# Attention scores of two heads at a time on two row halves of the array, queries turned two heads at a time

## The chip, the cores and the metric

The kernel runs on one core of one Trainium2 chip. The metric is the device time of one execution in microseconds (us), lower is better. Engines are named as in the profile: PE is TensorE's matmul, PEld its weight load, DVE is VectorE, ACT is ScalarE, POOL is GpSimd, SP is SyncE, which only issues DMAs here.

## The reference

One encoder layer on two sequences of 512 tokens, model width 1024. A normalised input is projected to queries (16 heads of 64), keys and values (4 heads of 64), the input of a state-space branch and two gates. The two branches are gated and added, an output projection and a squared-ReLU MLP follow. The change touches the attention branch alone:

```python
q = rms_norm(q.reshape(bsz, seq_len, N_HEADS, HEAD_DIM), q_gain)
k = rms_norm(k.reshape(bsz, seq_len, N_KV_HEADS, HEAD_DIM), k_gain)
...
s = jnp.einsum('nqkgd,njkd->nkgqj', qb, kw).astype(jnp.float32) * scale + bias
s = jnp.where(mask[:, None, None], s, NEG_INF)
sink_col = jnp.broadcast_to(sink_b, s.shape[:-1] + (1,))
p = jax.nn.softmax(jnp.concatenate([s, sink_col], axis=-1), axis=-1)[..., :-1]
o = jnp.einsum('nkgqj,njkd->nqkgd', p.astype(vs.dtype), vw)
```

A block of 128 queries sees its own block of keys and the two beside it, where they exist: two key blocks (256 keys) for the first and last block of a sequence, three (384 keys) for the two in the middle. A score is a product over 64 head dimensions.

## The kernel before

All matmuls split their float32 operands into a high and a low part of a faster type and add several products of the parts, so as to come near float32.

The attention stage (lines 953 to 1367) goes through 8 steps, one for each of the 4 key heads j and 2 sequences sq. A step has four units, one for each block qb of 128 queries. A unit covers the four query heads h = 0 to 3 that share key head j. Beside the unit, the step projects the queries of the next step, one tile of 128 tokens in each unit.

A tile of queries (class `Tile`) goes through these steps. `project` multiplies 24 products of 256 columns in portions. `square`, `power` and `norm` normalise each head: ScalarE squares (L1001), VectorE sums (L1005), POOL raises to the power -1/2 (L1007, L1008), VectorE multiplies into `qn` (L1012). In the kernel before, `qn` holds each head twice side by side, the second copy made by POOL (L1013). `turn` transposes each head's 128 columns (head twice) on TensorE (L1018), which gives 128 rows: the head's 64 dimensions, twice. `high` writes all 128 rows as the high part (L1023, ScalarE), and `low` writes rows 64 to 127 over with the low part (L1027, VectorE). So `queries[j, sq]` holds for each head the high part in rows 0 to 63 and the low part in rows 64 to 127.

Keys are treated alike once a step: `key_copies` (L972) makes two copies side by side on POOL, `key_turn` transposes them (L981) and writes a tile `kh` of high parts (L982) and a tile `kl` of low parts (L983), each with the same 64 dimensions in both row halves.

`scores(h)` then takes two matmuls of all 128 rows for a head (L1048): high and low queries against `kh`, and high and low queries against `kl`. Together these are all four products of the parts. The result is one PSUM bank from the pool `ps_s`, which has two banks, so the third head of a unit takes the bank of the first and the fourth that of the second.

`largest(h)` (L1052, VectorE) adds the bias, writes the scores to `p` and finds the negated row maximum; with it the score bank is free. Two instructions show in the profile: the custom operation and a read of its accumulator. `exp(h)` (L1058) is on ScalarE. The probabilities of a unit are used while the next unit runs (`prev`): `turn(i)` transposes the four heads' probabilities of key block i (L1064), `high(i)` (L1068, ScalarE) and `low(i)` (L1073, VectorE) split them, `value(i, part)` (L1080) multiplies with the values, `lower_part` (L1084) and, one unit later still, `add` (L1090, VectorE, two instructions) bring the output together.

The order on TensorE, ScalarE, VectorE and POOL is written out by hand (the manual schedule opened at L1195); an engine works off its instructions in that order. For the first part of a unit it is, in the kernel before: `scores(0)`, `largest(0)`, `rows.power`, `scores(1)`, `owed.add`, `largest(1)`, `prev.turn(0)`, `prev.high(0)`, 8 products of the projection, `prev.low(0)`, `exp(0)`, `exp(1)`, `rows.norm`, `scores(2)`, `largest(2)`, `prev.turn(1)`, `prev.high(1)`, 4 products, `value(0, 0)`, 2 products, `exp(2)`, `scores(3)`, a weight's low part, `prev.low(1)`, `value(0, 1)`, `largest(3)`, and then the third key block, 4 products, `rows.turn`, and the rest (lines 1217 to 1309). Here `rows` is the tile projected in the unit before, and `rows.turn` its transposes.

Of the kernel before, what the change touches and what calls it, by code (L numbers as in the profile page):

```python
# [11 lines left out]
F32 = mybir.dt.float32  # L12
F32R = mybir.dt.float32r
I32 = mybir.dt.int32
AF = mybir.ActivationFunctionType
ALU = mybir.AluOpType
AX = mybir.AxisListType

P = 128
# [6 lines left out]
HALF = 512  # L26
# [3 lines left out]
G = 4  # L30
HD = 64
# [32 lines left out]
def hybrid_layer(ctx, tc, x, xT, rel, onehot, early, w_qkv, w_ug, q_gain, k_gain, sink,  # L64
                 b_re, b_im, c_re, c_im, d_skip, w_glu, b_glu, w_out, ln2, w_up, w_down, out):
    nc = tc.nc
    V, S, PE, GP, SP = nc.vector, nc.scalar, nc.tensor, nc.gpsimd, nc.sync
# [12 lines left out]
    def acc():  # L80
        return ps_acc.tile([P, 512], F32, tag="acc", name="acc")

    def tps():
        return ps_t.tile([P, 512], F32, tag="tps", name="tps")

    def sps():
        return ps_s.tile([P, 512], F32, tag="sps", name="sps")
# [16 lines left out]
    ident = const.tile([P, P], F32, name="ident")  # L104
# [4 lines left out]
    gain_q = const.tile([P, 1], F32, name="gain_q")  # L109
# [161 lines left out]
    with tc.tile_pool(name="xin", bufs=2, reuse_waits="tile") as xin, tc.tile_pool(name="ssmc", bufs=1) as sc:  # L271
        def c64(name):
            return sc.tile([P, GROUPS], F32, tag=name, name=name)
# [65 lines left out]
        dt, mag, ang, kk = c64("dt"), c64("mag"), c64("ang"), c64("kk")  # L339
# [79 lines left out]
        for s in range(NSEQ):  # L419
            for c in range(3):  # L420
                out_ps[c, s] = (tps, tps, sps, sps, acc, lambda: ps_o.tile([P, 512], F32, tag="po", name="po"))[s * 3 + c]()
            for k in range(KT):
# [38 lines left out]
                for p, c in order:  # L461
                    PE.matmul(out_ps[c, s], u_w[c][p == 2][:, k, :], hT[s][p == 1][:, k, :],
                              start=k + p == 0, stop=k == KT - 1 and p == 1)
# [10 lines left out]
        for n in (1, 2, 4):  # L474
            a, b = slice(1, n + 1), slice(n + 1, 2 * n + 1)
# [46 lines left out]
    if True:  # L522
        h = hp.tile([P, NCHUNK, 2, GROUPS, NSEQ], F32, name="h")
# [429 lines left out]
    with tc.tile_pool(name="att", bufs=2, reuse_waits="tile") as ap:  # L953
        steps = [(j, sq) for j in range(N_KV) for sq in range(NSEQ)]
        weights, keys, queries, biases = {0: w_q0}, {}, {}, {}
# [12 lines left out]
                biases[j].append(bias)  # L968

        def key_copies(j, sq):  # L970
            kd = ap.tile([P, 4, 2, HD], F32, tag="qn", name="kd")
            GP.tensor_copy(kd, kn[:, sq * 4:sq * 4 + 4, j, None, :].to_broadcast([P, 4, 2, HD]))  # L972
            return kd

        def key_turn(j, sq, kd):
            kh = ap.tile([P, HALF], F32R, tag="kh", name="kh")
            kl = ap.tile([P, HALF], F32R, tag="kl", name="kl")
            keys[j, sq] = (kh, kl)
            ps = tps()
            for t in range(4):  # L980
                PE.transpose(ps[:, t * P:(t + 1) * P], kd[:, t].rearrange("p a d -> p (a d)"), ident)  # L981
            S.activation(kh, ps, AF.Copy, scale=gain_k)  # L982
            V.scalar_tensor_tensor(kl, ps, gain_k, kh.bitcast(F32), op0=ALU.mult, op1=ALU.subtract)  # L983
            queries[j, sq] = ap.tile([P, G, HALF], F32R, tag="qa", name="qa")

        class Tile:

# [20 lines left out]
                GP.tensor_tensor(self.rq, ms, neg_half[:, 0:G], op=ALU.pow)  # L1008

            def norm(self):  # L1010
                self.qn = ap.tile([P, G, 2, HD], F32, tag="qn", name="qn")
                V.tensor_mul(self.qn[:, :, 0], self.psv, self.rq[:, :, None].to_broadcast([P, G, HD]))  # L1012
                GP.tensor_copy(self.qn[:, :, 1], self.qn[:, :, 0])  # L1013

            def turn(self):
                self.pt = acc()
                for h in range(G):
                    PE.transpose(self.pt[:, h * P:(h + 1) * P], self.qn[:, h].rearrange("p a d -> p (a d)"), ident)  # L1018

            def high(self):  # L1020
                self.ptv = self.pt.rearrange("p (h t) -> p h t", h=G)
                self.dst = queries[self.key][:, :, self.t * P:(self.t + 1) * P]
                S.activation(self.dst, self.ptv, AF.Copy, scale=gain_q)  # L1023

            def low(self):
                dst = self.dst[64:128]
                V.scalar_tensor_tensor(dst, self.ptv[64:128], gain_q[64:128], dst.bitcast(F32),  # L1027
                                       op0=ALU.mult, op1=ALU.subtract)

        class Unit:  # L1030

# [9 lines left out]
                self.nmx = small.tile([P, G], F32, tag="nmx", name="nmx")  # L1041
                self.s, self.pt, self.hl = {}, {}, {}

            def scores(self, h):
                ps = self.s[h] = sps()
                qs = queries[self.j, self.sq][:, h, self.qb * P:(self.qb + 1) * P]
                for i, kk in enumerate(keys[self.j, self.sq]):
                    PE.matmul(ps[:, 0:self.nk], qs, kk[:, self.k0 * P:self.k1 * P], start=i == 0, stop=i == 1)  # L1048

            def largest(self, h):  # L1050
                hh, b0 = self.j * G + h, (self.k0 - self.qb + 1) * P
# [108 lines left out]
        def y_high(m, yr):  # L1160
            for s in range(NSEQ):
                S.copy(y_part(s, 0, m).rearrange("p (t k) -> p t k", t=T), yr[:, :, s, :])
# [36 lines left out]
        if True:  # L1199
            rows = entry()  # L1200
            for i, (j, sq) in enumerate(steps):
# [8 lines left out]
                for qb in range(NB):  # L1210
                    if 1 <= i < 3:

                        t = (i - 1) * NB + qb
# [3 lines left out]
                    cur = Unit(j, sq, qb, sums, ya)  # L1217
# [4 lines left out]
                    kd = None  # L1222
# [3 lines left out]
                        rows.power()  # L1226
                    if i == len(steps) - 1:
                        y_high(2 * qb, y_rows[2 * qb])
                    cur.scores(1)
                    if owed:  # L1230
                        owed.add()
                    cur.largest(1)
# [12 lines left out]
                    if qb == 0 and nxt:  # L1245
                        kd = key_copies(*nxt)
# [2 lines left out]
                        made = None  # L1249
                    if div:  # L1250
                        div.invert()
                    cur.scores(2)
                    cur.largest(2)
                    if i == len(steps) - 1:
                        y_low(2 * qb, y_rows[2 * qb])
# [7 lines left out]
                    if i == len(steps) - 1:  # L1263
                        y_high(2 * qb + 1, y_rows[2 * qb + 1])
                    cur.exp(2)
                    cur.scores(3)
                    if lower:
                        lower()
                        lower = None
# [632 lines left out]
    with tc.tile_pool(name="down0", bufs=2, side="right", reuse_waits="tile") as d0, \  # L1902
# [50 lines left out]
        ps = product_d(1)  # L1953
# [4 lines left out]
        ps = product_d(5, added(q3, q1, xq))  # L1958
# [5 lines left out]
        ps = product_d(6, added(q5, q5, xq))  # L1964
# [3 lines left out]
        ps = product_d(3)  # L1968
# [4 lines left out]
        ps = product_d(7)  # L1973
# [4 lines left out]
        ps = product_d(2, added(q1, q1, xq))  # L1978
# [3 lines left out]
        ps = product_d(4)  # L1982
# [77 lines left out]
```

## Time and profile before

| | us |
|---|---|
| three timed runs | 1470.78, 1468.74, 1468.35 |
| their median | 1468.74 |
| the profiled execution's own time: first to last instruction (span) | 1467.4 |
| TensorE busy in the span | 1446.3 |
| first to last start of a score matmul (L1048) | 451.4 to 675.3 |

The profiled execution is known by its span alone; the median of the timed runs lies 1.3 us above it, for what lies around the span and for the spread between runs. A row of a group names the line, engine, operation, written tile, read tiles, shape and count, then the busy time in us, the mean of one in ns, the idle time before it and what ended that. A row of the timeline begins with the start and the duration in us; several like instructions in a row are merged with their count, and then the duration runs from the first start to the last end. A matmul's duration is longer than the distance to the next matmul, since they are pipelined; the distance of two starts is what it costs TensorE.

### The profile page before, as it was taken

Reading aid. Unit: us, or ns where it says so; the run is one execution under the profiler, and the core shown is the slowest. Engines: PE = TensorE matmul, PEld = TensorE weight load, DVE = VectorE, ACT = ScalarE, POOL = GpSimd, SP = SyncE. Lnnn points to the kernel's source line nnn. Section 1 sums busy time; section 2 is a strip of 40 time slices with the busy share of each in tenths; the row PEclk is TensorE's granted clock in tenths of the full one; section 3 lists DMA queues with packets and bytes.
Section 4 is the critical chain, followed back from the end, with each engine's and each line's share of the span. In section 5 each row is a group of like instructions: output and inputs, shape, how many; then the busy total and the mean of one; then the engine's idle time right before and its main releaser. Section 6 shows DMA issues by size and latency. Waiting matters only on the chain.

```text
span 1467.4 us, 21580 instructions
## 1 busy us (share of the span) xinstructions
PE 1446.3 (99%) x7782; PEld 1234.1 (84%) x7782; DVE 1094.6 (75%) x1836; ACT 764.2 (52%) x1366; POOL 168.9 (12%) x270
## 2 busy tenths in 40 slices
PE   6999999999999999999999999999999999999998
PEld 5888888888999899987888888888888888888887
DVE  7799979975636889888974689877776588575653
ACT  5489862233426778787532355554554444333332
POOL 4111120000223333343101000000000000000000
PEclk9999999999999999999999999999999999999999
DMA  8355567259941413236964134544443894454441
GB/s 300 112 171 174 161 206 268 101 178 290 307 131 35 121 46 89 95 130 217 303 212 144 72 115 165 174 149 147 155 158 123 302 346 147 158 177 153 129 129 58
DMA packets 129239, 243.86 MB, mean 166 GB/s; under 512 B 16060, under 2 KB 59324, under 8 KB 129133
## 3 DMA queue, kind: packets, MB, share of 16 engines
q1 hardware_dynamic: 104684, 186.87, 40.4%
q10 hardware_dynamic: 21888, 46.15, 8.3%
q0 software_dynamic: 2560, 9.48, 2.0%
q8 instruction: 61, 1.00, 0.3%
q14 instruction: 46, 0.37, 0.1%
HBM read 173.20 MB, written 81.82 MB: 174 GB/s over the span
## 4 chain that ended last, share of the span: by engine, by line
PE 91%; DVE 3%; ACT 2%; DMA 1%; issue 1%; POOL 1%; SPq 0%; DVEq 0%; ACTq 0%; POOLq 0%
PE bank L115 14%; PE bank L116 14%; PE bank L117 14%; PE acc L141 11%; PE acc L724 8%; PE acc L753 5%; PE acc L115 3%; PE acc L117 3%; PE acc L116 3%; PE po L1080 2%; PE sps L604 2%; PE sps L1048 2%; PE sps L860 2%; PE tps L1064 2%; PE lag L619 1%
## 5 line engine op out<-in xcount | busy, mean ns | idle before, releaser
L116 PE MATMUL bank<-b_lo,a_hi 128*128 128x512 f32 x440 | 171.2, 389 | 0.0
L117 PE MATMUL bank<-b_hi,a_lo 128*128 128x512 f32 x440 | 171.2, 389 | 0.0
L115 PE MATMUL bank<-b_hi,a_hi 128*128 128x512 f32 x440 | 171.2, 389 | 0.0
L724 PE MATMUL acc<-w_hi,hT 128*128 128x256 f32 x768 | 165.0, 291 | 0.0
L141 PE MATMUL acc<-hT,c_hi 128*128 128x512 f32 x512 | 161.1, 394 | 0.0
L1933 ACT CAST a_hi<-d_a 128x1024 fp32r<-128x1024 f32 x55 | 58.0, 1054 | 178.1 <-PE bank L116 175.2
L1934 DVE TENSOR_TENSOR a_lo<-d_a,a_hi 128x1024 fp32r<-128x1024 f32 x55 | 67.3, 1223 | 99.4 <-ACT a_hi L1933 97.3
L724 PEld LDWEIGHTS acc<-w_hi,hT 128*128 128x128 f32 x768 | 126.7, 190 | 1.7
L141 PEld LDWEIGHTS acc<-hT,c_hi 128*128 128x128 f32 x512 | 94.6, 188 | 21.0 <-issue 2.5
L724 PE MATMUL acc<-w_lo,hT 128*128 128x256 f32 x384 | 108.2, 282 | 0.0
L141 PE MATMUL acc<-hT,c_lo 128*128 128x512 f32 x256 | 100.3, 392 | 0.0
L115 PE MATMUL bank<-act,u_hi 128*128 128x512 f32 x256 | 99.6, 389 | 0.0
L116 PE MATMUL bank<-act,u_hi 128*128 128x512 f32 x256 | 99.6, 389 | 0.0
L117 PE MATMUL bank<-act,u_lo 128*128 128x512 f32 x256 | 99.6, 389 | 0.0
L117 PEld LDWEIGHTS bank<-b_hi,a_lo 128*128 128x128 f32 x440 | 82.6, 188 | 17.3
L115 PEld LDWEIGHTS bank<-b_hi,a_hi 128*128 128x128 f32 x440 | 82.6, 188 | 17.1
L116 PEld LDWEIGHTS bank<-b_lo,a_hi 128*128 128x128 f32 x440 | 82.6, 188 | 17.1
L1058 ACT ACTIVATE p<-p,nmx 128x257 f32<-128x257 f32 (+1 forms) x128 | 72.1, 564 | 27.0 <-DVE nmx L1052 24.3
L724 PEld LDWEIGHTS acc<-w_lo,hT 128*128 128x128 f32 x384 | 73.0, 190 | 2.5
L1052 DVE CUSTOM_DVE_ANT_0 p<-sps,bias,nsink 128x256 f32<-128x256 f32 (+1 forms) x128 | 69.2, 541 | 2.9 <-PE sps L1048 0.4
L1717 ACT CAST u_hi<-s 128x512 fp32r<-128x512 f32 x64 | 39.3, 621 | 59.8 <-PE bank L116 43.1
L1934 DVE TENSOR_TENSOR b_lo<-k,b_hi 128x1024 fp32r<-128x1024 f32 x55 | 66.9, 1217 | 0.0
(387 smaller groups left out, 3622.9 us busy)
## 6 DMA issues: line engine op xcount, KB each, us to landing
d_a<-a_scr SPq DMA_DIRECT2D x55, 512.0 KB, 3.6
u_raw<-in_w_up_dram SPq DMA_DIRECT2D x32, 512.0 KB, 5.7
a_scr<-t ACTq DMA_DIRECT2D x64, 256.0 KB, 2.1
k<-in_w_down_dram SPq DMA_DIRECT2D x32, 512.0 KB, 5.7
a_scr<-a ACTq DMA_DIRECT2D x48, 256.0 KB, 3.3
c_raw<-in_w_ug_dram SPq DMA_DIRECT2D x44, 256.0 KB, 3.6
ct_scr<-ctab SPq DMA_DIRECT2D x16, 576.0 KB, 3.3
ctab_in<-ct_scr SPq DMA_DIRECT2D x32, 288.0 KB, 4.7
```

Of the source, the lines that this page charges most:

```text
L115: PE.matmul(ps, a[0], b[0], start=first, stop=False)
L116: PE.matmul(ps, a[0], b[1], start=False, stop=False)
L117: PE.matmul(ps, a[1], b[0], start=False, stop=last)
L141: PE.matmul(self.ps[s], self.w[p == 2][:, k, :], hT[s][p == 1][:, k, :], start=i % (3 * KT) == 0, stop=i % (3 * KT) == 3 * KT - 1)
L604: PE.matmul(ps[:, i * P:(i + 1) * P], bm[:, ri, g, :], u_sb[:, g, :], start=True, stop=True)
L724: PE.matmul(ps, act[p == 2][:, k, col:col + P], self.w[k // 4][p == 1][:, k % 4, :], start=i == 0, stop=i == 3 * KT - 1)
L753: PE.matmul(self.ps[s], w_g[self.m][p == 2][:, k, :], y_part(s, int(p == 1), k), start=k + p == 0, stop=k == KT - 1 and p == 2)
L1052: V.tensor_tensor_reduce(self.p[:, h, 1:1 + self.nk], self.s[h][:, 0:self.nk], biases[self.j][h][:, b0:b0 + self.nk], -1.0, nsink[:, hh:hh ...
L1058: S.activation(p, p, AF.Exp, bias=self.nmx[:, h:h + 1], scale=-1.0, accum_out=self.sums[:, h, self.qb:self.qb + 1])
L1717: S.copy(hi, src)
L1933: S.copy(hi, src)
L1934: V.tensor_sub(lo, src, hi.bitcast(F32))
```

## The change

Queries are no longer doubled. `norm` writes the four heads side by side, without POOL's copy. `turn` transposes two heads at once, so that a tile of queries takes two transposes instead of four; head 2m comes into rows 0 to 63 and head 2m + 1 into rows 64 to 127. `high` and `low` write two separate tiles of this form, each 128 rows by 256 columns. `scores(m)` now makes the scores of the heads 2m and 2m + 1: three products of 64 rows for each head (high queries with high keys, low with high, high with low), the two heads alternating, head 2m in the rows 0 to 63 of the array and head 2m + 1 in the rows 64 to 127, into two score banks. The product of the two low parts is left out.

In the written order, `scores(0)` stands where `scores(0)` stood, and covers heads 0 and 1. `scores(1)` stands where `scores(2)` stood, and covers heads 2 and 3. Nothing else is moved. The key copies have one buffer (`bufs=1`) in the place of two shared with the queries.

```diff
         def key_copies(j, sq):
-            kd = ap.tile([P, 4, 2, HD], F32, tag="qn", name="kd")
+            kd = ap.tile([P, 4, 2, HD], F32, tag="qn", name="kd", bufs=1)
...
-            queries[j, sq] = ap.tile([P, G, HALF], F32R, tag="qa", name="qa")
+            queries[j, sq] = ap.tile([P, 2, 2, HALF], F32R, tag="qa", name="qa")
...
             def norm(self):
-                self.qn = ap.tile([P, G, 2, HD], F32, tag="qn", name="qn")
-                V.tensor_mul(self.qn[:, :, 0], self.psv, self.rq[:, :, None].to_broadcast([P, G, HD]))
-                GP.tensor_copy(self.qn[:, :, 1], self.qn[:, :, 0])
+                self.qn = ap.tile([P, G, HD], F32, tag="qm", name="qn")
+                V.tensor_mul(self.qn, self.psv, self.rq[:, :, None].to_broadcast([P, G, HD]))
 
             def turn(self):
-                self.pt = acc()
-                for h in range(G):
-                    PE.transpose(self.pt[:, h * P:(h + 1) * P], self.qn[:, h].rearrange("p a d -> p (a d)"), ident)
+                self.pt = acc()[:, 0:2 * P]
+                for m in range(2):
+                    PE.transpose(self.pt[:, m * P:(m + 1) * P], self.qn[:, 2 * m:2 * m + 2].rearrange("p a d -> p (a d)"), ident)
 
             def high(self):
-                self.ptv = self.pt.rearrange("p (h t) -> p h t", h=G)
-                self.dst = queries[self.key][:, :, self.t * P:(self.t + 1) * P]
-                S.activation(self.dst, self.ptv, AF.Copy, scale=gain_q)
+                self.ptv = self.pt.rearrange("p (m t) -> p m t", m=2)
+                self.hi, self.lo = [queries[self.key][:, i, :, self.t * P:(self.t + 1) * P] for i in range(2)]
+                S.activation(self.hi, self.ptv, AF.Copy, scale=gain_q)
 
             def low(self):
-                dst = self.dst[64:128]
-                V.scalar_tensor_tensor(dst, self.ptv[64:128], gain_q[64:128], dst.bitcast(F32),
-                                       op0=ALU.mult, op1=ALU.subtract)
+                V.scalar_tensor_tensor(self.lo, self.ptv, gain_q, self.hi.bitcast(F32), op0=ALU.mult, op1=ALU.subtract)
...
-            def scores(self, h):
-                ps = self.s[h] = sps()
-                qs = queries[self.j, self.sq][:, h, self.qb * P:(self.qb + 1) * P]
-                for i, kk in enumerate(keys[self.j, self.sq]):
-                    PE.matmul(ps[:, 0:self.nk], qs, kk[:, self.k0 * P:self.k1 * P], start=i == 0, stop=i == 1)
+            def scores(self, m):
+                for e in range(2):
+                    self.s[2 * m + e] = sps()
+                tok, kk = slice(self.qb * P, (self.qb + 1) * P), slice(self.k0 * P, self.k1 * P)
+                for n, (a, b) in enumerate(((0, 0), (1, 0), (0, 1))):
+                    for e in range(2):
+                        rows_ = slice(e * 64, (e + 1) * 64)
+                        PE.matmul(self.s[2 * m + e][:, 0:self.nk], queries[self.j, self.sq][rows_, a, m, tok],
+                                  keys[self.j, self.sq][b][rows_, kk], start=n == 0, stop=n == 2)
...
-                    cur.scores(1)
                     if owed:
                         owed.add()
                     cur.largest(1)
...
-                    cur.scores(2)
+                    cur.scores(1)
                     cur.largest(2)
...
                     cur.exp(2)
-                    cur.scores(3)
```

## The prediction

> **What bounds the kernel now.** I first read the busy shares of the page, then the same shares for the stretch in which the attention steps run, 460 to 640 us, since the change touches nothing outside attention.
>
> ```profile
> span 1467.4 us, 21580 instructions
> PE 1446.3 (99%) x7782; PEld 1234.1 (84%) x7782; DVE 1094.6 (75%) x1836; ACT 764.2 (52%) x1366; POOL 168.9 (12%) x270
> ...
> 460.00:640.00 180.00, 178.66 (x1310) 166.28 (x1311) 157.83 (x418) 143.69 (x364) 63.50 (x113) 1.00 0.27 80
> ```
>
> The columns of the last line are PE, PEld, DVE, ACT, POOL, clock, DMA. TensorE is busy for 178.66 of 180 us; VectorE comes second with 157.83, or 88%. So TensorE time taken out of this stretch would come off the span, but only while VectorE keeps up, and its slack is about one part in eight. The waits of the same stretch say where VectorE already holds TensorE up:
>
> ```profile
> PEld sps L1048 <- DVE nmx L1052: 2.1, 7, 0.7
> ```
>
> The 128-row score products (L1048) wait 2.1 us in 7 cases for VectorE's row maximum (L1052), because that frees a score bank. There are only two such banks (`ps_s`, bufs=2). This small wait is the one that the change enlarges, so the order of TensorE and VectorE inside a unit (one head group, one block of 128 queries) has to be read next. Here is a unit with two key blocks (256 score columns, "narrow"), TensorE first, then VectorE:
>
> ```profile
> 594.96 0.28 PE L1048 MATMUL sps<-kh,qa 128*128 128x256 f32 x1
> ...
> 596.83 0.28 PE L1048 MATMUL sps<-kh,qa 128*128 128x256 f32 x1
> ```
>
> ```profile
> 594.57 0.76 DVE L1027 SCALAR_TENSOR_TENSOR qa<-acc,gain_q,qa 64x512 fp32r<-64x512 f32 x1 [0.41 <-ACT qa L1023]
> 595.40 0.49 DVE L1052 CUSTOM_DVE_ANT_0 p<-sps,bias,nsink 128x256 f32<-128x256 f32 x1
> 595.81 0.08 DVE L1052 DVE_READ_ACCUMULATOR2_ANT nmx<- 128x1 f32 x1
> 595.81 0.41 DVE L1005 TENSOR_REDUCE ms<-sq 128x4 f32<-128x256 f32 x1
> 596.14 0.84 DVE L1090 TENSOR_TENSOR ya<-po,ol 64x256 f32<-64x256 f32 x2
> 597.01 0.49 DVE L1052 CUSTOM_DVE_ANT_0 p<-sps,bias,nsink 128x256 f32<-128x256 f32 x1
> 597.42 0.08 DVE L1052 DVE_READ_ACCUMULATOR2_ANT nmx<- 128x1 f32 x1
> 597.42 0.69 DVE L1073 TENSOR_TENSOR pl<-tps,ph 128x512 fp32r<-128x512 f32 x1
> ```
>
> Heads 0 and 1 are scored from 594.96 on, two products each. Their banks come free at 595.81 + 0.08 = 595.89 and 597.42 + 0.08 = 597.50: between the two maxima stand a reduce and two adds. Head 2 is scored at 596.83 and needs only head 0's bank. Head 1's bank is still taken then, for another 0.67 us, and nobody minds, as head 3 is scored later. A unit with three key blocks (384 columns, "wide"):
>
> ```profile
> 523.68 0.34 PE L1048 MATMUL sps<-kh,qa 128*128 128x384 f32 x1
> ...
> 525.76 0.34 PE L1048 MATMUL sps<-kh,qa 128*128 128x384 f32 x1
> ```
>
> ```profile
> 524.41 0.62 DVE L1052 CUSTOM_DVE_ANT_0 p<-sps,bias,nsink 128x384 f32<-128x384 f32 x1
> ...
> 526.69 0.08 DVE L1052 DVE_READ_ACCUMULATOR2_ANT nmx<- 128x1 f32 x1
> ```
>
> Here head 1's bank comes free at 526.77, 1.01 us after head 2's start.
>
> **The change part by part.** There are 32 units (4 head groups, 2 sequences, 4 blocks), 16 narrow and 16 wide, and 32 query tiles.
>
> *Turning the queries.* Two transposes (L1018) a tile instead of four; the gain mul (L1012) writes half the tile, and the copy on POOL (L1013) goes.
>
> ```profile
> 593.05 0.44 PE acc L1018 x4
> ...
> 594.67 0.46 PE po L1080 x2
> 595.13 0.47 PE sps L1048 x4
> ...
> 601.61 0.70 PE sps L1048 x4
> ...
> L1023 ACT ACTIVATE qa<-acc,gain_q 128x512 fp32r<-128x512 f32 x32 | 21.6, 675 | 0.1
> L1001 ACT ACTIVATE sq<-acc 128x256 f32<-128x256 f32 x32 | 12.0, 375 | 10.6 <-PE acc L724 10.6
> L983 DVE SCALAR_TENSOR_TENSOR kl<-tps,gain_k,kh 128x512 fp32r<-128x512 f32 x8 | 6.0, 750 | 11.1 <-ACT kh L982 11.1
> L1012 DVE TENSOR_TENSOR qn<-acc,rq 128x256 f32<-128x256 f32 x32 | 13.3, 415 | 2.2 <-POOL rq L1008 2.1
> ```
>
> In the chain of work four transposes take 0.44, so two less save 0.22 a tile, 7.0 in all. The high part shrinks from 675 ns (L1023) to about the 375 ns of a 128x256 activation. The low part goes from 64x512 (0.76) to 128x256: between L983's 750 and L1012's 415 ns, nearest the latter because of the shape. These free ScalarE and VectorE near the end of a unit. In the narrow unit above, the low part ends at 595.33, and head 0's second product, one slot of 0.12 (below) behind the first, is complete at 594.96 + 0.12 + 0.28 = 595.36: VectorE is in time for the maximum anyway, so there the relief is worth nothing. In units where it comes later it lets the maxima start on time. I count that below by starting every unit's maximum when its scores are there. The key copy's single buffer (`kd`, bufs=1) is asked for once in four units, long after its transposes; I cost it at nothing, and a late copy would stall the key turn by at most its POOL time, once a step. No DMA is issued, dropped or moved, on SP's queue or POOL's.
>
> *The score products.* Two heads take 4 products of 128 rows now; then 6 of 64 rows, in 3 pairs on two row halves. No row of this trace shows two row halves. The nearest are matmuls on two column halves, where the lag table is made (L619 alternates output partitions 0 and 64):
>
> ```profile
> 150.79 0.50 PE L604 MATMUL sps<-u_sb,bm 128*128 128x128 f32 x3
> 151.22 0.33 PE L619 MATMUL lag<-ctab,lbt 128*48 128x144 f32 x2
> ...
> 151.22 0.17 PEld L619 LDWEIGHTS lag<-ctab,lbt 128*48 128x48 f32 x4
> ...
> 151.87 0.54 PE L619 MATMUL lag<-ctab,lbt 128*48 128x144 f32 x6
> 152.34 0.73 PE L141 MATMUL acc<-hT,c_hi 128*128 128x512 f32 x2
> ```
>
> The first two L619 matmuls fit into 0.33 us, about what one takes: the halves run side by side, and their loads too. So bounds per pair of products are one slot (side by side) and two slots (one after another); I take one. A slot is 0.47 / 4 = 0.12 narrow and 0.70 / 4 = 0.175 wide (the L1048 rows of the chain above). The six products then take 0.36 or 0.525, against 0.47 or 0.70.
>
> *Going into halves and back.* The same rows show a gap. The third L604 starts at 150.79 + 2 x 0.11 = 151.01, and at that pace L619 would start at 151.12; it starts at 151.22, 0.10 late. On the way back the last pair starts at 151.87 + 0.54 - 0.29 = 152.12; pairs are 0.12 apart, so 152.24 was due, and it is 152.34, 0.10 late. The second L141 starts 0.73 - 0.39 = 0.34 after the first, where a 512-column product takes 0.46 / 2 = 0.23 (the chain's L1080): its predecessor had no weights in place, 0.11 more. A crossing costs about 0.2 us, bounds 0 (if row halves need none) and 0.21. There are four a unit. I take 0.2, because the trace's only split of the array shows it both ways.
>
> [...]
>
> *The moved scores.* Heads 0 and 1 are scored together as before. Heads 2 and 3 are now scored where head 2 was, so this group needs head 1's bank as well: the wait that nobody minded becomes TensorE's own. Behind the waiting product stand, in TensorE's order, the transposes of probabilities, 4 projection products, and the value products; ScalarE's casts and VectorE's maximum of head 2 wait for them. VectorE has the low part (L1073, 0.69) and the norm (L1012, 0.41) in between, longer than the group's three slots, so it doesn't run dry.
>
> Per unit, without crossings: head 0's third product starts two slots after the unit's start. Narrow: 2 x 0.12 + 0.28 = 0.52, and the maximum starts 0.04 later (595.40 after 595.36), 0.56. From there to head 1's bank it takes 597.50 - 595.40 = 2.10, and as much again, 0.04, to hand over: 2.70. TensorE's second group now starts 596.83 - 594.96 = 1.87 after the unit's start, so it comes 0.83 later. What the first group saves is lost in the wait. Behind it TensorE saves one slot (0.12) and two transposes (0.22). Net +0.49. Wide: 2 x 0.175 + 0.34 + 0.04 = 0.73; 526.77 - 524.41 = 2.36; with the hand-over 3.13 against 525.76 - 523.68 = 2.08, so 1.05 later; saved 0.175 and 0.22; net +0.65. In the 7 cases of the waits view, 2.1 us of this is waited already.
>
> Sum: 16 x 0.49 + 16 x 0.65 - 2.1 = 16.1. The first two units have no adds in front of head 1's maximum (0.84 each): -1.7. The tile turns of the opening part have no such wait (3 x 0.22 saved), and three units of the last step have no tile to turn (3 x 0.22 not saved): these cancel. That is +14.4. Of the four crossings a unit, the way out of the first group and the way into the second lie inside the wait; the other two count: 32 x 2 x 0.2 = +12.8. Total +27.2, so 1467.4 becomes 1494.6. The median of the timed runs lies 1.3 above the span, so I forecast **1496 us**.
>
> **The rivals.** *A, no gap for row halves.* The pairs run side by side and the crossings cost nothing. For it: no row of the trace shows row halves alone. Against: both ends of L619. 1468.7 + 14.4 = 1483.
>
> *B, the change doesn't do what it says: the halves run one after another.* Head 0's last product is then the fifth, two slots later, and behind the wait five products are left instead of three: four slots a unit, 16 x 4 x (0.12 + 0.175) = +18.9. With 14.4 that is +33.3, 1502 without crossings and 1515 with them. Against it: L619's pairs.
>
> *C, faster: the second group needn't wait.* If VectorE had head 1's bank free when TensorE comes, TensorE's own work alone would count: 32 x (0.12 + 0.175) = 9.4 and 7.0 of transposes, 16.4 saved, 1452. The place is the second group's first product into head 1's bank. It decides at 16.4 / 32 = 0.51 us a unit: a shorter wait, with no gaps, makes the kernel faster. With one slot less in the first group TensorE would arrive 1.87 - 0.12 = 1.75 after a narrow unit's start and finds the bank free at 2.70, 0.95 later; in a wide one at 2.08 - 0.175 = 1.9 and 3.13, 1.2 later. So the wait would have to be half of what the rows give, and there must be no gaps. For it: VectorE and ScalarE get shorter work.
>
> *D, loads that can't run ahead.* If the weights of a row half can't be loaded while that half multiplies, the second and third pair of each group show their load, 0.11 as at 152.34. One pair before head 0's end (two loads, 0.22) and two behind the wait count: 32 x 0.44 = 14 more, 1510. The third and fourth load of L619 begin by 151.22 + 0.17 - 0.12 = 151.27, while the first two matmuls run, which speaks against it. [...]
>
> **How the numbers follow.** The forecast (side by side, with gaps) has 55%, A 20%, B 12%, D 5%, C 8% (5 faster, 3 at no change, where the wait is just halved). Forecast, A, D and B without gaps lie between 1479 and 1510, with a few us for units that differ from my two; left out are B with gaps and C, and some of A's and D's edges. Faster by over 0.2% (2.9 us, about what a measurement of this kernel can tell from no change) 5%, within it 3%, slower 92%.
>
> **What would show it right or wrong.** Right: waits of TensorE or its loads at the score products for L1052 rise from 2 us to some 20 to 30 us; the third product of a pair starts within some 0.01 us of its twin; gaps of 0.1 us with no releaser stand before a unit's first scores and behind its second group; VectorE's and ScalarE's shares fall in a longer stretch. Wrong: if the second group starts as early as head 2 did (C), if pairs are a slot apart (B), if the product behind a group follows at the usual pace (A), or if VectorE begins the maxima later than its scores are there, which would add to every unit.

## The result, and the profile after

The changed kernel takes 1502.47 us (median of 4 runs, 1500.28 to 1503.76) against 1469.38 us (4 runs, 1468.35 to 1470.78) before: a ratio of 1.0223 [1.0208, 1.0237]. It is slower, as forecast, and 6.5 us longer than the forecast. The profiled execution has a span of 1502.0 us, 34.6 more than the 1467.4 of before; its run took 1503.76.

The page of the changed kernel, span and busy shares:

```profile
span 1502.0 us, 21622 instructions
...
PE 1461.3 (97%) x7846; PEld 1225.3 (82%) x7846; DVE 1089.6 (73%) x1836; ACT 758.9 (51%) x1366; POOL 154.0 (10%) x238
```

The stretch from 460 to 640 us of the changed kernel (columns: PE, PEld, DVE, ACT, POOL, granted clock, DMA share, GB/s):

```profile
460.00:640.00 180.00, 162.29 (x1163) 136.27 (x1161) 130.62 (x354) 120.21 (x312) 44.35 (x73) 0.97 0.25 72
```

TensorE, busy for 178.66 of these 180 us before, now stands still for nearly 18. VectorE falls from 157.83 to 130.62 and ScalarE from 143.69 to 120.21: no engine has taken over as the bound, so something must be waited for. The waits of the changed kernel between 450 and 720 us (engine, tile and line, what it waited for: us in total, times, longest):

```profile
PEld sps L1048 <- DVE nmx L1053: 19.8, 30, 1.4
PE sps L1048 <- DVE nmx L1053: 13.1, 27, 1.2
POOL ya L1120 <- DMA y_scr<-y_scr: 15.3, 1, 15.3
...
DVE qn L1012 <- POOL rq L1008: 12.0, 3, 10.5
...
PEld acc L1017 <- DVE qn L1012: 8.5, 1, 8.5
```

The first two rows are the wait that the prediction names, about once in each of the 32 units. (A load and its product wait at the same time, as for head 3 below, where the load goes at 555.85 and the product at 555.86, so the two totals aren't added.) The other three each hold one long case, and nothing in the prediction speaks of them. These are two different events, and they are read one after the other.

**The wait at the second group.** A narrow unit of the changed kernel, TensorE and then VectorE:

```profile
552.72 0.40 PE L1081 MATMUL po<-pl,va 128*128 128x512 f32 x1
553.05 0.51 PE L1048 MATMUL sps<-kh,qa 64*128 64x256 f32 x4
553.39 0.28 PE L1048 MATMUL sps<-kl,qa 64*128 64x256 f32 x2
553.60 0.66 PE L1065 MATMUL tps<-ident,p 128*128 128x128 f32 x4
...
554.93 0.28 PE L724 MATMUL acc<-w_lo,hT 128*128 128x256 f32 x1
555.15 0.38 PE L1048 MATMUL sps<-kh,qa 64*128 64x256 f32 x1
555.86 0.50 PE L1048 MATMUL sps<-kh,qa 64*128 64x256 f32 x3 [0.32 <-DVE nmx L1053]
```

```profile
553.70 0.48 DVE L1053 CUSTOM_DVE_ANT_0 p<-sps,bias,nsink 128x256 f32<-128x256 f32 x1 [0.87 <-PE sps L1048]
...
554.11 0.41 DVE L1005 TENSOR_REDUCE ms<-sq 128x4 f32<-128x256 f32 x1
554.44 0.83 DVE L1091 TENSOR_TENSOR ya<-po,ol 64x256 f32<-64x256 f32 x2
555.31 0.48 DVE L1053 CUSTOM_DVE_ANT_0 p<-sps,bias,nsink 128x256 f32<-128x256 f32 x1
555.72 0.08 DVE L1053 DVE_READ_ACCUMULATOR2_ANT nmx<- 128x1 f32 x1
```

Head 2's first product starts at 555.15, and head 3's, which needs head 1's bank, only at 555.86, 0.06 after the bank comes free at 555.72 + 0.08 = 555.80. The reduce (0.41) and two adds (0.83) between the maxima are the ones shown in the prediction. From the unit's start it is 555.86 - 553.05 = 2.81 us; 2.70 were forecast, and 0.10 of the difference is the later start of the group's second pair, told next.

**The crossings.** The last value product at 552.72 fills 0.23, so the first pair was due at 552.95; it starts at 553.05, 0.10 late. Four products take 0.51: with 0.28 for one, the second pair starts 0.23 after the first, where later pairs are 0.12 apart. So another 0.10 goes by. The loads (PEld) of the first pair start with its products at 553.05, those of the second pair at 553.16 and those of the third at 553.27, 0.11 to 0.12 ahead of their products; that the 0.10 is the time of a load is my estimate from these starts. On the way back the last pair (553.39) leaves room for the transposes at 553.51, and they start at 553.60, 0.09 late.

**The long unit.** One unit alone, the last of step 1, takes 17.98 us from its first score to the next unit's, where units of its kind take 7.9. The order of transfers on SP's queue, before:

```profile
493.14 0.33 SPq L1109 DMA_DIRECT2D rs_scr<-row  x1
493.58 0.83 SPq L717 DMA_DIRECT2D w_raw<-in_w_qkv_dram  x2
494.46 0.53 SPq L1214 DMA_DIRECT2D y_scr<-y_scr  x1
495.10 1.28 SPq L1114 DMA_DIRECT2D fac<-rs_scr  x2
503.96 1.95 SPq L966 DMA_DIRECT2D bias<-line_scr  x2
```

And after:

```profile
493.72 0.33 SPq L1110 DMA_DIRECT2D rs_scr<-row  x1
504.21 1.92 SPq L966 DMA_DIRECT2D bias<-line_scr  x2
506.23 0.38 SPq L717 DMA_DIRECT2D w_raw<-in_w_qkv_dram  x1
506.71 1.29 SPq L1115 DMA_DIRECT2D fac<-rs_scr  x2
```

The two loads of `bias` now stand ahead of the two of `fac`. The first bias load starts only at 504.21, 0.03 after a head's maximum has ended (504.10 + 0.08) and set a bias tile free, SP waits 10.4 us for VectorE ahead of it, and `fac` waits behind both: it is issued at 506.71 instead of 495.10. The manual schedule orders PE, ACT, DVE and POOL; SP isn't in it: the framework's planner orders its transfers, and for this kernel it chose another order. What hangs on `fac` shows on POOL and TensorE of the changed kernel, with the clock beside it (the columns of the last fence as above):

```profile
512.99 2.34 POOL L1120 TENSOR_TENSOR ya<-ya,fac 128x1024 f32<-128x1024 f32 x1 [15.26 <-DMA y_scr<-y_scr]
...
515.86 1.04 POOL L1008 TENSOR_TENSOR rq<-ms,neg_half 128x4 f32<-128x4 f32 x1
```

```profile
517.41 0.69 PE L1017 MATMUL acc<-ident,qn 128*128 128x128 f32 x2 [8.27 <-DVE qn L1012]
```

```profile
503.04:508.90 5.86, 5.52 (x45) 4.80 (x44) 2.66 (x8) 1.19 (x3) 0.00 (x0) 1.00 0.46 110
509.10:517.20 8.10, 0.04 (x1) 0.00 (x0) 0.27 (x1) 1.56 (x5) 3.89 (x5) 0.73 0.58 174
517.40:519.20 1.80, 1.79 (x8) 1.70 (x9) 1.66 (x6) 1.41 (x4) 0.00 (x0) 0.50 0.31 79
```

POOL's multiply of the outputs by `fac` waits 15.26 us. The row names the y_scr transfer that stands behind `fac` in the queue, but what POOL waited for is `fac`: its second load is issued at 507.40 and the two loads took 5.2 us to land, so it is there at about 512.6, while y_scr, issued at 508.05 and 5.9 us on its way, lands only after the multiply has begun. The power for the next tile's norm stands behind it in POOL's written order, VectorE's norm behind the power, and the query transposes behind the norm hold all of TensorE for 8.27 us. When it starts again, its clock is granted at 0.50. So of the 10.1 us that this unit takes too long, 8.27 are the stall, and about 1.8 more are an estimate of what the clock costs: the 3.6 us from 517.41 to the next unit's start at half pace.

**The sum, by the starts of the score groups.** From the start of the kernel to the first score: -1.15. Step 0: +1.23. Step 1: +11.17. Steps 2 to 6: +16.81 (31.70 against 28.34 a step). Step 7 up to its last unit: +2.99. Behind that: +3.5. Together +34.6. The long unit is 17.98 - 7.9 = 10.1 of it; the other units and the edges are 24.5, where the terms of the forecast came to 27.2.

### The profile page after: what moved, and what is told of

It reads as the page before. It is cut to its first block, busy times and chain, and to the rows that moved or that the text cites. A ratio compares the mean times of both kernels' runs of the same rounds, so it can differ in the third digit from the quotient of the medians.

```text
span 1502.0 us, 21622 instructions
## 1 busy us (share of the span) xinstructions
PE 1461.3 (97%) x7846; PEld 1225.3 (82%) x7846; DVE 1089.6 (73%) x1836; ACT 758.9 (51%) x1366; POOL 154.0 (10%) x238
## 4 chain that ended last, share of the span: by engine, by line
PE 86%; DVE 5%; DMA 3%; issue 2%; ACT 1%; POOL 1%; SPq 0%; DVEq 0%; POOLq 0%; ACTq 0%
PE bank L117 13%; PE bank L116 13%; PE bank L115 13%; PE acc L141 11%; PE acc L724 7%; PE acc L115 3%; PE acc L117 3%; PE acc L116 3%; PE acc L753 3%; PE sps L1048 2%; PE po L1081 2%; PE sps L604 2%; PE sps L860 2%; PE tps L1065 2%; DVE p L1053 1%
## 5 line engine op out<-in xcount | busy, mean ns | idle before, releaser
L724 PE MATMUL acc<-w_hi,hT 128*128 128x256 f32 x768 | 165.9, 293 | 0.0
L724 PEld LDWEIGHTS acc<-w_hi,hT 128*128 128x128 f32 x768 | 127.4, 191 | 2.0
L724 PE MATMUL acc<-w_lo,hT 128*128 128x256 f32 x384 | 108.6, 283 | 0.0
L724 PEld LDWEIGHTS acc<-w_lo,hT 128*128 128x128 f32 x384 | 73.5, 191 | 2.4
L1074 DVE TENSOR_TENSOR pl<-tps,ph 128x512 fp32r<-128x512 f32 x80 | 55.0, 689 | 16.7 <-ACT ph L1069 16.1
```

Source lines behind the costliest of these rows:

```text
L724: PE.matmul(ps, act[p == 2][:, k, col:col + P], self.w[k // 4][p == 1][:, k % 4, :], start=i == 0, stop=i == 3 * KT - 1)
L1074: V.tensor_sub(pl, self.pt[i], self.hl[i][0].bitcast(F32))
```

## The experiments

Each was measured beside the kernel before on the same chip. "Units" are distances between the first scores of units in the steady steps 2 to 6, for the blocks qb 0 to 3; where one number stands for a block, it is the median of its five.

**1 and 2. SP's order.** The first experiment writes SP's order out by hand in step 1, from its second unit on; the second also issues `fac` where it was issued before.

```diff
+                    if i == 1 and qb == 1:
+                        held = tc.manual_schedule(engines={mybir.EngineType.SP})
+                        held.__enter__()
...
+                if i == 1:
+                    held.__exit__(None, None, None)
```

> The changed kernel, with SP's transfers of the second step kept in the order of the program, so that the two loads of the division factors (fac) stand ahead of all loads of the next bias rows, as in the kernel before. Theory, SP order: in the changed kernel the fac loads stood behind a bias load that waited for a free buffer; POOL's multiplication waited for them, and behind it the power of the next query tile, its norm and its transposes on TensorE; one unit took 17.98 us where its like take 7.9. Then this kernel takes 10 us less than the changed one, about 1492, and that unit 7.9. Rival: the transfers themselves were slow or POOL waited for another thing; then the unit stays near 18 us and the time at 1502.

Measured: 1497.96 us, ratio 1.0185 [1.017, 1.0201]. That is only half of the 10 us. The bias loads are out of the way, but a weight piece now stands behind `fac`, and ScalarE waits for it. The waits of this kernel from 493 to 508 us:

```profile
ACT w_hi L718 <- DMA w_raw<-in_w_qkv_dram: 5.4, 1, 5.4
```

One unit earlier is long now (13.31, where 8.5 is usual). So the loss goes with the queue, but the written order wasn't that of before. In the second experiment the two loads of `fac` are issued one unit later, behind the y2 transfer:

```diff
+                if (j, sq) != (0, 0):
+                    self.factors()
+
+            def factors(self):
...
+                        if i == 1 and qb == 2:
+                            made.factors()
```

> The changed kernel, with SP's transfers of the second step held in an order close to that of the kernel before: the row of sums, a weight piece, a state-space transfer, the factor loads (fac), then further pieces and the bias rows. In the first try the factors came ahead of the weight piece; the long unit fell from 17.98 to 13.31 us instead of 8.5, because ScalarE now waited 5.4 us for the weight piece. Theory, SP order: with both early no unit of the second step is over 8.6 us, and the time is about 9 to 10 us below the changed kernel's 1502.5, 1491 to 1494. Rival, the transfers are too slow in any order (the state-space transfer of 512 KB lies beside them): the unit stays 4 us or more too long, 1497.

Measured: 1492.98 us, ratio 1.0155 [1.014, 1.017], 9.5 us below the changed kernel, with only SP's order and the place of the two loads altered. The longest unit of step 1 is 9.40, above the 8.6 that was expected, since a weight piece is still waited for (2.6). The order of the transfers, then, costs at least 9.5 us.

**3. Both maxima first.** `largest(1)` is moved ahead of the tile's power and the adds. It is the changed kernel in all else.

```diff
                     cur.largest(0)
+                    cur.largest(1)
                     if rows and not rows.qn:
                         rows.power()
...
                         owed.add()
-                    cur.largest(1)
```

> The changed kernel with VectorE's maximum of head 1 moved ahead of the reduce and the two adds. The same sums are made in another order. SP's transfers have the order of the kernel before again. Theory, wait and crossings: head 1's bank is free 1.2 us earlier, the wait at the second score group goes, and what is left against the kernel before is four crossings of 0.2 us a unit (25.6) less the 16.4 us that TensorE saves in products and transposes: 1478, within 1475 to 1483. Rival 1, crossings cost nothing: 1453. Rival 2, the wait is not what costs: only the 10 us of the SP order come off, 1492.

Measured: 1470.71 us, ratio 1.0 [0.9991, 1.0009]. The waits of this kernel between 450 and 720 us, and the second group of a narrow unit with VectorE's maxima:

```profile
PEld sps L1048 <- issue: 6.1, 19, 0.4
...
PEld sps L1048 <- DVE nmx L1053: 0.5, 2, 0.2
```

```profile
563.34 0.51 PE L1048 MATMUL sps<-kh,qa 64*128 64x256 f32 x4
...
565.42 0.51 PE L1048 MATMUL sps<-kh,qa 64*128 64x256 f32 x4
```

```profile
563.99 0.48 DVE L1053 CUSTOM_DVE_ANT_0 p<-sps,bias,nsink 128x256 f32<-128x256 f32 x1 [0.86 <-DMA bias<-line_scr]
...
564.80 0.09 DVE L1053 DVE_READ_ACCUMULATOR2_ANT nmx<- 128x1 f32 x1
```

Head 1's bank is free at 564.89, half a microsecond before TensorE comes (565.42), and its four products with `kh` go without a wait. The wait is gone but for 0.5 us; what stays are short gaps before score products that no semaphore explains ("issue"), on the way into the halves. Steps 2 to 6 fall from 31.70 to 28.26 us, 0.86 a unit, and SP's order is that of before again, so that the long unit vanishes too (8.96). Yet the result is not faster than before, and it came 4 us below the bottom of what was expected: something that saves time is missing in the forecast (see below).

**4. The wait alone.** In the kernel before, without row halves, the scores of head 3 are moved to stand directly behind head 2's.

```diff
                     cur.scores(2)
+                    cur.scores(3)
                     cur.largest(2)
...
                     cur.exp(2)
-                    cur.scores(3)
```

> The kernel before with one edit: the scores of head 3 are made directly behind those of head 2, so the bank wait comes without row halves and without other turns. Theory, wait: TensorE stands still from head 2's end until head 1's maximum is done, by the kernel before 0.7 us in a narrow unit and 0.8 to 1.05 in a wide one: 1468.7 plus about 25, 1490 to 1497. Rival, the wait is taken up by slack later in the unit: 1469 to 1474.

Measured: 1486.52 us, ratio 1.0111 [1.0096, 1.0126]; 3.5 us below the range expected. The waits of this kernel between 450 and 720 us, and a narrow unit's second group:

```profile
PEld sps L1048 <- DVE nmx L1052: 26.6, 38, 1.4
```

```profile
575.11 0.28 PE L1048 MATMUL sps<-kl,qa 128*128 128x256 f32 x1
575.72 0.39 PE L1048 MATMUL sps<-kh,qa 128*128 128x256 f32 x1 [0.33 <-DVE nmx L1052]
```

Head 3's first product was due at 575.23 and goes at 575.72, 0.49 late. The 0.7 that was expected is the time from head 2's start to the free bank (0.67 in the prediction's unit), but head 2's own two products fill 0.24 of it. Steps 2 to 6 grow by 2.76 us each, 0.69 a unit, and step 1 only by 0.55. The wait needs nothing of the new layout; pulling two heads' scores together is enough.

**5. The heads of the second group apart.** In the changed kernel, head 2's products stay where the second group was, and head 3's go behind `exp(2)`, where head 3 was scored before.

```diff
-                    cur.scores(1)
+                    cur.scores(1, (0,))
                     cur.largest(2)
...
                     cur.exp(2)
+                    cur.scores(1, (1,))
```

> The changed kernel with the scores of head 2 and of head 3 apart, each in the place that it had before, three products of 64 rows one behind the other; heads 0 and 1 stay a pair. No bank wait is left; SP's transfers have the order of the kernel before. A unit has 9 slots of products in place of 8 (0.15 more), six crossings in place of none, and two transposes less (0.22). Theory, a crossing costs 0.2 us: +1.13 a unit, 36 in 32 units, 1505. [...] Rival 2, no cost: 1466.

Measured: 1491.01 us, ratio 1.0144 [1.0127, 1.0161], between the numbers that were expected. The wait is down to 1.6 us in all, but there are six slots in the place of three, and two crossings more. Against experiment 3, which has next to no wait either, a steady unit takes 0.80 more. Three slots are 3 x (0.12 + 0.175) / 2 = 0.44, which leaves 0.36 for two crossings, 0.18 each.

**6. One group cut in two.** To price a crossing by itself, experiment 3 is taken, and the transposes of probabilities that stand behind the second group are put between its first pair and the other two. The work stays the same, with two crossings more.

```diff
-                    cur.scores(1)
+                    cur.scores(1, (0,))
+                    if n3:
+                        prev.turn(1)
+                    cur.scores(1, (1, 2))
                     cur.largest(2)
...
-                        prev.turn(1)
```

> The version with the early maximum (max_first, 1470.7), with the four 128-row transposes of probabilities that stand behind the second score group moved between its first pair and the other two. No work is added; two crossings are added in 31 units. Theory, a crossing costs 0.12 to 0.2 us: 7.4 to 12.4 more, 1478 to 1483. Rival, a crossing costs nothing and the 20 us of the version with heads apart have another cause: 1471.

Measured: 1478.09 us, ratio 1.0054 [1.0039, 1.0069], 7.4 us above experiment 3. A narrow unit of it on TensorE:

```profile
570.65 0.38 PE L1049 MATMUL sps<-kh,qa 64*128 64x256 f32 x2
570.97 0.66 PE L1066 MATMUL tps<-ident,p 128*128 128x128 f32 x4
571.55 0.39 PE L1049 MATMUL sps<-kh,qa 64*128 64x256 f32 x2
571.77 0.28 PE L1049 MATMUL sps<-kl,qa 64*128 64x256 f32 x2
```

The pair alone holds TensorE from 570.65 to 570.97, where a slot is 0.12. From the start of the group to the first projection product behind it, it takes 571.98 - 570.65 = 1.33 us; in experiment 3 it took 566.39 - 565.42 = 0.97. Steady units grow by the same 0.36 us: 0.18 for each crossing, as in experiment 5. (In 31 units that is 11 us; the two profiled executions differ by 10.3, and the one of experiment 3 was among its fastest, 1467.81 against a median of 1470.71, so the medians differ by less.)

**7. Product order head by head.** Experiment 3 again, with all three products of head 2m written ahead of the three of head 2m + 1. If TensorE took them in order, only the products at the seam would lie side by side.

```diff
-                for n, (a, b) in enumerate(((0, 0), (1, 0), (0, 1))):
-                    for e in range(2):
-                        rows_ = slice(e * 64, (e + 1) * 64)
+                for e in range(2):
+                    rows_ = slice(e * 64, (e + 1) * 64)
+                    for n, (a, b) in enumerate(((0, 0), (1, 0), (0, 1))):
```

> The version with the early maximum (max_first, 1470.7), with the products of a group ordered head by head: three of head 2m, then three of head 2m + 1. Theory, the halves run side by side in pairs: now only the third product of the one and the first of the other can overlap, 5 slots instead of 3 in each group, 2 x 2 x 0.147 = 0.59 us a unit, 19 in 32 units: 1489. Rival 1, a half never runs beside the other: no change, 1471. Rival 2, nothing overlaps in this order: 6 slots, 28 more, 1499.

Measured: 1470.23 us, ratio 1.0001 [0.9992, 1.001], the time of experiment 3. By the expectation this would mean that the halves don't lie side by side at all. The trace of this kernel says otherwise:

```profile
565.03 0.51 PE L1048 MATMUL sps<-kh,qa 64*128 64x256 f32 x4
565.37 0.29 PE L1048 MATMUL sps<-kl,qa 64*128 64x256 f32 x2
```

The order written is kh, kh, kl, kh, kh, kl, and the starts in the trace are four times kh, then twice kl, in pairs 0.01 us apart. In this trace the second half doesn't wait for the first half's product with `kl`, so the written order made no difference, and this experiment couldn't tell what it was made for. The pairs themselves answer the question.

**8 to 10. Fewer crossings, and the long unit shortened.** In experiment 8 a narrow unit scores all four heads in one group, two heads in each bank (2 x 256 columns); wide units stay as in experiment 3.

```diff
+                if self.nkb == 2:
+                    if m:
+                        return
+                    for e in range(2):
+                        bank_ = sps()
+                        for mm in range(2):
+                            self.s[2 * mm + e] = bank_[:, mm * 2 * P:(mm + 1) * 2 * P]
+                    self.products(0)
+                    return self.products(1)
```

> The version with the early maximum (max_first, 1470.7), with all four heads of a narrow unit scored in one group: two heads share a bank, 256 columns each, and the pairs still lie in different banks. Two crossings less in 16 units. Theory, 0.12 to 0.2 us a crossing: 3.8 to 6.4 less, 1464 to 1467, under the kernel before. Rival, the next unit now waits for head 3's maximum and gives it back: 1471 or more.

Measured: 1468.75 us, ratio 0.9995 [0.9984, 1.0005]. Narrow units fall from 6.71 to 6.52 and from 7.18 to 7.00, by 0.18 to 0.19 where two crossings at 0.18 would be 0.36. What takes up the other half isn't shown. One unit of step 1 takes 9.18, where SP still has two weight pieces (from 490.56) behind the store of the row sums (490.12), which waits for ScalarE (14.9 us in the kernel before). In experiment 9, ScalarE issues that store itself:

```diff
-                self.queue.dma_start(rs_scr[sq, j * G:(j + 1) * G, :].rearrange("h (b t) -> (h b) t", b=NB), row)
+                (GP if self.last else S).dma_start(rs_scr[sq, j * G:(j + 1) * G, :].rearrange("h (b t) -> (h b) t", b=NB), row)
```

> The version with all four heads of a narrow unit in one group, with the store of the row sums (rs_scr) issued by ScalarE, which has made the row, instead of standing in SP's queue ahead of the weight pieces. In that version one unit of the second step took 9.18 us where its like take 7.58, behind a weight piece that SP issued only after the row. Theory, SP's queue: that unit falls to under 8 us, 1.2 to 1.6 us come off, 1467 against 1469.8 before, 0.997 to 0.999. Rival, the weight piece is slow itself because the state-space transfer lies beside it: no change, 1469.

Measured: 1467.05 us (12 runs) against 1469.42 (23 runs), ratio 0.9981 [0.9972, 0.9991]; the long unit falls to 7.58. This is the one version that beats the kernel before, by 0.19%. Experiment 10 makes the same edit of the store in the kernel before:

> The kernel before with the same edit: the row sums' store issued by ScalarE. There the unit of the second step took 8.38 us where its like take 7.4. Theory, SP's queue: up to 1 us comes off, 1468.8, which is inside the spread of the runs. Rival: ScalarE's issue delays its own work and the time rises by 1 us or more.

Measured: 1470.43 us, ratio 1.0006 [0.9997, 1.0014]. The unit falls from 8.38 to 7.70, but the other wide units without a key turn grow from 7.41 to about 7.7, and nothing is left. So the gain of experiment 9 isn't that of the store alone.

## Why the prediction was right or wrong

The median steady unit of each block, in us:

| block | before | forecast change | change | both maxima first | wait alone | first maximum starts, before | in the changed kernel |
|---|---|---|---|---|---|---|---|
| qb 0, narrow | 6.48 | +0.89 | +0.95 | +0.23 | +0.58 | 0.44 | 0.65 |
| qb 1, wide, behind a key turn | 7.34 | +1.05 | +0.44 | -0.52 | +0.97 | 1.61 | 0.91 |
| qb 2, wide | 7.41 | +1.05 | +1.10 | +0.16 | +0.77 | 0.73 | 0.83 |
| qb 3, narrow | 7.13 | +0.89 | +0.77 | +0.05 | +0.42 | 1.03 | 0.65 |

The forecast is its net wait with two crossings (0.49 + 0.4, 0.65 + 0.4), ahead of the small corrections; the next three columns are differences from the kernel before. The last two are the time from a unit's first score to VectorE's first maximum. The prediction read one unit of qb 0 and one of qb 2, and for these two blocks it is within 0.06; it misses in the other two.

*The wait: right.* It stands where the prediction put it, at head 1's bank, with its length within 0.11 of the forecast in the unit shown. Taken away (experiment 3) it gives back 0.86 a unit in steps 2 to 6; put in alone (4) it costs 0.69.

*Pairs side by side: right*, one slot a pair. Rival B, one half after the other, falls by the starts of the pairs (0.01 apart), and D, loads that can't run ahead, by the third pair: its loads start at 553.27, with the products of the second, and it comes at the usual pace of 0.12. Only the second pair comes late, 0.23 after the first.

*The crossings: right*, 0.18 measured in two ways against 0.2 taken from the column halves of L619. Rival A, no gap for row halves, falls by experiment 6 (0.36 for two crossings). At the two ends of a group of row halves stand gaps of 0.10 and 0.09 (before 553.05 and 553.60). What a crossing costs in all is measured by experiments 5 and 6.

*Rival C* needed both: no wait, and no gaps. Experiment 3 has the first without the second and lands on the time of before. So the gaps alone use up all that fewer slots, fewer transposes and the relief told below save.

*"No DMA is issued, dropped or moved, on SP's queue or POOL's": wrong.* This is the step that failed. The change itself touches no transfer, but the planner sorted SP's queue anew, and two loads that wait for a buffer came ahead of two that were urgent. At least 9.5 us (experiment 2) are missing in the forecast; with them, 1496 would have been 1505.5.

*The relief of VectorE and ScalarE: too small.* The prediction starts every maximum of the changed kernel when its scores are there, but compares that with two units in which the maximum was on time before, so that the relief comes out as nothing. Experiment 3 is the measure: TensorE saves a slot in each group (0.295 a unit) and two transposes (0.22), 0.51, and pays four crossings, 0.72, so it should be 0.21 slower a unit; it is 0.02 faster. About 0.23 a unit, some 7 us in all, is relief that the forecast doesn't have. By the table it lies in qb 1 and qb 3, the two blocks in which VectorE came late to its first maximum before. A unit of qb 1 begins at 573.07 in the kernel before and at 592.09 in the changed one; VectorE, before and after:

```profile
573.90 0.76 DVE L1027 SCALAR_TENSOR_TENSOR qa<-acc,gain_q,qa 64x512 fp32r<-64x512 f32 x1 [0.32 <-ACT qa L1023]
574.69 0.62 DVE L1052 CUSTOM_DVE_ANT_0 p<-sps,bias,nsink 128x384 f32<-128x384 f32 x1
```

```profile
592.59 0.48 DVE L1025 SCALAR_TENSOR_TENSOR qa<-acc,gain_q,qa 128x256 fp32r<-128x256 f32 x1
592.99 0.61 DVE L1053 CUSTOM_DVE_ANT_0 p<-sps,bias,nsink 128x384 f32<-128x384 f32 x1
```

The queries' low part stands right before the maximum both times. It waits 0.32 for ScalarE's high part and takes 0.76 before, doesn't wait and takes 0.48 after, and the maximum starts 0.90 after the first score in place of 1.62. The waits of TensorE's loads in the unit before, 573.07 to 580.44 us:

```profile
PEld po L1080 <- DVE pl L1073: 0.3, 1, 0.3
PEld sps L1048 <- DVE nmx L1052: 0.2, 1, 0.2
```

In experiment 3 TensorE waits for VectorE in none of these places. So the term that was mis-sized is the wide unit's +1.05 applied to the 8 units of qb 1, where +0.44 was measured. That the shorter query parts are the whole of the relief is argued from these rows, not shown: no experiment shortened them alone.

The two errors have opposite signs: units and edges came to 24.5 in place of 27.2, and the queue added about 10. That the forecast came within 6.5 us is in part luck. The range, 1479 to 1510, held for the mechanism that it was made for, but a part of its upper end was used up by an event that it didn't contain.

## What to carry to other kernels

Here, pulling two consumers of a double buffer together turned the later of the two buffer releases into a wait, 0.69 us a unit by itself (experiment 4); with the release, VectorE's second maximum, moved forward as well, 0.5 us of it was left in the whole stage (experiment 3). So look for such a wait at the place where the second consumer used to stand. Where the array is split, count both ends of every split group: at 0.18 us each (experiments 5 and 6), four of them, 0.72, used up more than the two slots and two transposes, 0.51, that they paid for. And after any edit read the order of every queue that isn't written by hand: here loads that nobody touched changed places, and behind one that waited 10.4 us for a buffer `fac` was issued at 506.71 in place of 495.10.

## What the runs showed that was not expected

*In experiment 7 the two row halves don't keep to the written order among each other.* The second half's two products with `kh` start 0.01 us after those of the first half, ahead of the first half's product with `kl`, which is written before them. That an engine works off its instructions in the written order doesn't hold for these starts.

*The stall cost more than its length.* In the changed kernel the granted clock falls while TensorE stands still: it is 1.00 up to 512 us, 0.94 in the next microsecond and 0.50 from 513 us on. After the 8.27 us TensorE goes on at half pace:

```profile
520.03 0.63 PE L1081 MATMUL po<-ph,va 128*128 128x512 f32 x1
520.46 0.63 PE L1081 MATMUL po<-pl,va 128*128 128x512 f32 x1
...
523.22 0.40 PE L724 MATMUL acc<-w_hi,hT 128*128 128x256 f32 x2
```

These two start 0.43 apart, where a product of 512 columns took 0.23 before. The pace is back at 523.22, where two L724 products take 0.40 again. So a stretch of some 5.7 us behind the stall ran at the slow clock as well (0.51 from 517.40 to 523.20), and the unit that begins in it takes 7.82 us, where its like take 7.43.
